# V and the scaled output rows of an RWKV-7 stage turned by 128x128 transpositions, with VectorE moving quarter blocks between the halves of the rows

## The chip, the cores and the metric

The kernel runs on one core of one Trainium2 chip. The metric is the device time of one execution in microseconds. The kernel before took 2906.01 us, the median of three runs from 2901.53 to 2912.75.

## What is computed

The reference is a decoder block on 512 positions of width 2048: RWKV-7 time mixing with 16 heads of 64 beside sliding-window attention, both merged by gates, then a gated convolutional feed-forward part. Only the time mixing is touched here. In the lines that matter, `v` is the value row of a head and `y` the state's output, which is centred and scaled per head and position:

```python
    def step(state, inp):
        r_t, k_t, v_t, w_t, ka_t, kb_t = inp
        sa = jnp.einsum('bhvk,bhk->bhv', state, ka_t)
        state = (state * w_t[:, :, None, :] + sa[..., None] * kb_t[:, :, None, :]
                 + v_t[..., None] * k_t[:, :, None, :])
        y = jnp.einsum('bhvk,bhk->bhv', state, r_t)
        return state, y
...
    mu = jnp.mean(y, axis=-1, keepdims=True)
    var = jnp.mean(jnp.square(y - mu), axis=-1, keepdims=True)
    y = ((y - mu) * lax.rsqrt(var + GN_EPS)).reshape(B, S, RW_DIM)
    y = y * gn_w.astype(f32) + gn_b.astype(f32)
```

`y` is linear in `v` along the head's columns, so the kernel takes the mean away from V at the start, and the mean of `y` is then zero.

## The kernel before

The program has four stages: projections of the input (`w_z`), with attention and the time mixing running beside them; the branch product; the output product (`w_out`); and the feed-forward part. The time mixing lies between about 330 and 1165 us. It works on eight pairs of heads, 128 rows each: `early(p)` makes the rows of a pair from three projections (k, r, v), `late(p)` runs the recurrence in eight chunks of 64 positions, and `final(p)` normalises the output and writes it out. They are called as late(p), early(p+1), final(p), then three projections for the gates.

Every projection is 48 matmuls of 128x512 (L262, L263, L264: high and low parts of the weights by high and low parts of the input). ScalarE makes the high part of a weight tile (`whi`, L245), VectorE the low part (`wlo`, L246); three buffers of each are in turn. These matmuls depend on nothing in the time mixing, and the framework's scheduler puts them between the time mixing's own instructions wherever it reckons that those would have to wait. In this text such matmuls are called filling. Each engine executes its queue in the order that the scheduler wrote; an instruction that waits holds all behind it.

Steps of one pair that the change touches:

- In `late`, ScalarE copies the halves of `vz` (128 channels x 512 positions) into the off-diagonal halves of `BV` (L668). Eight f32 products of 128x64 with the constant `cens` (an identity less 1/64) turn the chunks and centre them at once (L717 through `bulk_mm`, L714), and ScalarE copies the result from PSUM into `VV` (L715): positions of a chunk in the rows, channels in the columns, the head 1 of the pair in rows 0 to 63 and the head 0 in rows 64 to 127. Each f32 product of this kind shows as two MATMUL records in the trace.
- The next step, `GV` (L719, L714), needs `VV` and `OA`. Ahead of it on VectorE stand the masks of the chunk products (L694, sixteen of 128x256), and then, for each half g of the chunks, `tt` (L698, L699), `at_` (L705), the split into `AI` and `XIW` (L209) and `BT` (L710). `bulk` is a pool of three PSUM banks that all these products take in turn.
- In `final`, ScalarE copies y out of PSUM (`yt`, L802) and squares it (L808); VectorE sums (L810), takes the reciprocal root in thirteen small steps on 128x8 (`rsqrt_small`, L192 to L199), masks it for the two heads (`rs2`, L813), and makes two products of 128x512 (`yd`, L817). Eight f32 products with the constant `istack1` turn `yd` back (L820). Then come two products for the gate (L598), and VectorE finishes (L822, L825).

```python
                bulk_mm(VV, lambda n: BV[:, n], lambda n: K["cens"])
                GV = wk.tile([P, NCH, C], F32, name="GV", tag="yt")
                bulk_mm(GV, lambda n: OA[:, n], lambda n: VV[:, n])
```

## Time and profile before

| what | value |
|---|---|
| median of three runs | 2906.01 us |
| time of the profiled execution | 2907.66 us |
| its span | 2905.8 us |
| granted TensorE clock | 0.996 |
| TensorE (matmul) busy | 2850.9 us, 98% |
| VectorE busy | 1934.3 us, 67% |
| ScalarE busy | 1314.6 us, 45% |

A row of the timeline has the start in us, the time, the engine, the line, the operation, its operands and shapes, how many were merged, and in brackets the idle time ahead and what ended it. The time of a single matmul contains its way through the array; what a row of matmuls costs the queue is the distance from its start to the start of the next row. PE is TensorE, DVE VectorE, ACT ScalarE.

### The profile page before, as it was taken

The numbers are of one execution on the slowest core, as the hardware profiler recorded it, in microseconds if no ns is written. First come the engines' busy times: TensorE is split into PE (matmuls) and PEld (weight loads), VectorE is DVE, ScalarE is ACT, GpSimd is POOL, SyncE is SP. The second block draws the span as 40 slices with busy tenths as digits, with TensorE's granted clock in tenths as the row PEclk, the third lists the DMA queues.
The fourth block names the chain that finished last, engine by engine and source line by source line (L and its number), as shares of the span: only waits on it lengthen the run. The fifth ranks groups of instructions, "written<-read, shape, count | busy, mean of one in ns | idle before, by whom it ended". The sixth has DMA issues, their size and how long they took to land.

```text
span 2905.8 us, 47150 instructions
## 1 busy us (share of the span) xinstructions
PE 2850.9 (98%) x18162; PEld 2491.5 (86%) x18162; DVE 1934.3 (67%) x3314; ACT 1314.6 (45%) x2196; POOL 228.4 (8%) x304
## 2 busy tenths in 40 slices
PE   7999999999999999999999899999999999999999
PEld 6777778878878878788888899999999999888887
DVE  5555676666667665355668778777787777665555
ACT  4344344344334434322356455555555555544444
POOL 0001000000000000111000101110110100000000
PEclk9999999999999999999999999999999999999999
DMA  6855666566665666978787888888888888877775
GB/s 189 213 153 141 171 154 167 147 167 148 160 160 142 161 160 158 282 225 257 270 258 215 224 221 225 241 239 221 235 226 239 241 224 236 308 241 239 259 256 189
DMA packets 223729, 607.38 MB, mean 209 GB/s; under 512 B 24448, under 2 KB 44560, under 8 KB 222480
## 3 DMA queue, kind: packets, MB, share of 16 engines
q1 hardware_dynamic: 156096, 432.92, 45.9%
q0 software_dynamic: 36064, 132.14, 23.9%
q10 hardware_dynamic: 31344, 39.31, 3.9%
q8 instruction: 142, 2.33, 0.3%
q14 instruction: 83, 0.68, 0.1%
HBM read 554.66 MB, written 174.40 MB: 251 GB/s over the span
## 4 chain that ended last, share of the span: by engine, by line
PE 90%; DMA 4%; DVE 4%; issue 1%; ACT 1%; SPq 0%; DVEq 0%; ACTq 0%; POOLq 0%
PE X L1129 17%; PE X L996 10%; PE acc L263 10%; PE acc L262 10%; PE acc L264 10%; PE Y L996 8%; PE Y L1129 8%; PE Z L1129 4%; PE bulk L714 1%; PE bulk L770 1%; PE bulk L740 1%; PE bulk L690 1%; DMA raw<-in_w_up_dram 1%; PE mi L503 1%; PE acc L325 1%
## 5 line engine op out<-in xcount | busy, mean ns | idle before, releaser
L262 PE MATMUL acc<-xhi,whi 128*128 128x512 f32 x1120 | 453.6, 405 | 4.7 <-ACT whi L245 4.7
L264 PE MATMUL acc<-xhi,wlo 128*128 128x512 f32 x1120 | 451.5, 403 | 2.8 <-DVE wlo L246 2.8
L263 PE MATMUL acc<-xlo,whi 128*128 128x512 f32 x1120 | 453.0, 404 | 0.0
L245 ACT ACTIVATE whi<-raw 128x512 fp32r<-128x512 f32 x352 | 220.3, 629 | 499.2 <-PE acc L263 369.0
L246 DVE TENSOR_TENSOR wlo<-raw,whi 128x512 fp32r<-128x512 f32 x352 | 241.4, 689 | 233.5 <-ACT whi L245 227.7
L989 DVE TENSOR_TENSOR wlo<-raw,whi 128x1024 fp32r<-128x1024 f32 x210 | 257.0, 1224 | 205.4 <-ACT whi L988 204.3
L988 ACT ACTIVATE whi<-raw 128x1024 fp32r<-128x1024 f32 x210 | 222.6, 1060 | 291.4 <-PE X L996 152.5
L1129 PE MATMUL X<-b,whi 128*128 128x256 f32 x1472 | 269.1, 283 | 2.2 <-DVE u L1149 0.9
L1129 PE MATMUL X<-t,whi 128*128 128x256 f32 x1408 | 259.9, 285 | 9.9 <-DVE u L1149 9.4
L1112 DVE TENSOR_TENSOR wlo<-raw,whi 128x1024 fp32r<-128x1024 f32 x176 | 215.0, 1222 | 77.3 <-ACT whi L1111 77.0
L1129 PE MATMUL Y<-t,whi 128*128 128x256 f32 x1408 | 257.1, 283 | 0.0
L262 PEld LDWEIGHTS acc<-xhi,whi 128*128 128x128 f32 x1120 | 211.9, 189 | 44.4 <-ACT whi L245 5.5
L264 PEld LDWEIGHTS acc<-xhi,wlo 128*128 128x128 f32 x1120 | 211.9, 189 | 42.0 <-DVE wlo L246 4.0
L263 PEld LDWEIGHTS acc<-xlo,whi 128*128 128x128 f32 x1120 | 211.8, 189 | 37.3 <-issue 1.8
L1111 ACT ACTIVATE whi<-a 128x1024 fp32r<-128x1024 f32 x132 | 139.4, 1056 | 216.5 <-DVE a L1105 214.5
L1129 PEld LDWEIGHTS X<-b,whi 128*128 128x128 f32 x1472 | 229.5, 192 | 3.0 <-issue 2.3
L1129 PEld LDWEIGHTS X<-t,whi 128*128 128x128 f32 x1408 | 221.8, 194 | 10.5 <-DVE u L1149 6.9
L1129 PEld LDWEIGHTS Y<-t,whi 128*128 128x128 f32 x1408 | 219.6, 192 | 0.0
L1129 PE MATMUL X<-b,wlo 128*128 128x256 f32 x736 | 208.5, 283 | 2.1 <-DVE wlo L1112 2.1
L1112 DVE TENSOR_TENSOR wlo<-a,whi 128x1024 fp32r<-128x1024 f32 x132 | 161.7, 1225 | 67.6 <-ACT whi L1111 67.0
L1129 PE MATMUL X<-t,wlo 128*128 128x256 f32 x704 | 200.4, 285 | 0.0
L1129 PE MATMUL Y<-t,wlo 128*128 128x256 f32 x704 | 199.2, 283 | 0.0
(769 smaller groups left out, 6007.1 us busy)
## 6 DMA issues: line engine op xcount, KB each, us to landing
raw<-in_w_up_dram SPq DMA_DIRECT2D x180, 512.0 KB, 4.9
raw<-in_w_z_dram SPq DMA_DIRECT2D x288, 256.0 KB, 4.0
s_dn<-in_w_dn_dram POOLq DMA_DIRECT2D x88, 512.0 KB, 6.5
raw<-in_w_up_dram POOLq DMA_DIRECT2D x88, 512.0 KB, 8.4
raw<-s_dn SPq DMA_DIRECT2D x88, 512.0 KB, 4.1
raw<-in_w_dn_dram SPq DMA_DIRECT2D x66, 512.0 KB, 3.6
a<-in_w_up_dram SPq DMA_DIRECT2D x48, 512.0 KB, 4.4
s_dn<-in_w_dn_dram SPq DMA_DIRECT2D x44, 512.0 KB, 4.7
```

What stands on the lines that cost most here:

```text
L245: pin(act.activation(hi, raw, AF.Copy))
L246: pin(dve.tensor_tensor(lo, raw, hi.bitcast(F32), op=ALU.subtract))
L262: pe.matmul(acc, whi[:, j], xhi[:, k], start=first, stop=False)
L263: pe.matmul(acc, whi[:, j], xlo[:, k], start=False, stop=False)
L264: pe.matmul(acc, wlo[:, j], xhi[:, k], start=False, stop=last)
L325: pin(pe.matmul(heads[i][:, hs], l, r[:, k, hs], start=h == 0 and k + j == 0, stop=k == NK - 1 and j == 2, skip_group_check=True))
L988: act.activation(whi, wr, AF.Copy)
L989: dve.tensor_tensor(wlo, wr, whi.bitcast(F32), op=ALU.subtract)
L996: pe.matmul(dst, l[:, q, ts], r[:, es], start=fst and j == 0, stop=lst and j == 2, skip_group_check=True)
L1111: pin(act.activation(hi, t, AF.Copy))
L1112: pin(dve.tensor_tensor(lo, t, hi.bitcast(F32), op=ALU.subtract))
L1129: pin(pe.matmul(ps, l[:, k], r[:, k], start=start and k + i == 0, stop=last and i == 2, skip_group_check=True))
```

## The change

V: four transpositions of 128x128 turn `vz` as it stands, so that `BV`, its copies and its clearing go. A transposed block has 128 positions, that is two chunks, in its rows, and both heads in its columns. VectorE sums the 64 columns of each head and position out of PSUM (`vm`, 128x8), multiplies by -1/64, and adds that in four operations of 64x4x64, each of which reads one half of the rows of PSUM and writes one half of the rows of `VV`. In two of the four the halves differ.

Output: the mask `rs2` goes. Four operations of 64x4x64 instead of two of 128x512 make `yd`, now with 128 positions in the rows and both heads in the columns; again two of the four move between the halves. Four transpositions of 128x128 turn it back, instead of eight products. The constants `istack1` and `cens` go.

```diff
-                    act.activation(BV[hs, :, ol:oh], vz3[hs], AF.Copy)
...
-                bulk_mm(VV, lambda n: BV[:, n], lambda n: K["cens"])
+                ps = bulk()
+                for t in range(NT):
+                    ts = slice(t * P, (t + 1) * P)
+                    pe.transpose(ps[:, ts], vz[:, ts], ident)
+                vm = wk.tile([P, NCH], F32, name="vm", tag="vm")
+                dve.reduce_sum(vm, r3(ps), axis=AX.X)
+                dve.tensor_scalar(vm, vm, -1.0 / HD, None, op0=ALU.mult)
+                for a, (fl, fh) in enumerate(HV):
+                    for h in range(2):
+                        ol, oh = HV[1 - h]
+                        dve.tensor_tensor(VV[ol:oh, a::2], r3(ps)[fl:fh, h::2],
+                                          vm[fl:fh, h::2].unsqueeze(2).to_broadcast([C, NT, C]), op=ALU.add)
...
-                rs2 = wk.tile([P, NCH, 2], F32, name="rs2", tag="rs2")
-                dve.tensor_tensor(rs2, rs.unsqueeze(2).to_broadcast([P, NCH, 2]),
-                                  K["sel2"].unsqueeze(1).to_broadcast([P, NCH, 2]), op=ALU.mult)
-                yd = wk.tile([P, NCH, 2, C], F32, name="yd", tag="ko")
-                for h in range(2):
-                    dve.tensor_tensor(yd[:, :, h], yt, rs2[:, :, h : h + 1].to_broadcast([P, NCH, C]), op=ALU.mult)
+                yd = wk.tile([P, NT, 2, C], F32, name="yd", tag="ko")
+                for a, (al, ah) in enumerate(HV):
+                    for h, (lo, hi) in enumerate(HV):
+                        dve.tensor_tensor(yd[al:ah, :, h], yt[lo:hi, a::2],
+                                          rs[lo:hi, a::2].unsqueeze(2).to_broadcast([C, NT, C]), op=ALU.mult)
                 ps = bulk()
-                for n in range(NCH):
-                    pe.matmul(r3(ps)[:, n], yd[:, n].rearrange("p h c -> p (h c)"), K["istack1"], start=True, stop=True)
+                for t in range(NT):
+                    pe.transpose(ps[:, t * P : (t + 1) * P], yd[:, t].rearrange("p h c -> p (h c)"), ident)
```

The scheduler orders the engines anew. Three places around the start of the third pair follow (the output step is that of the second pair, which ends just ahead of it); line numbers of the changed kernel are smaller by two to five up to `late` and larger by five to six behind it (L694 becomes L689, L714 becomes L709, L820 becomes L825).

TensorE at V, before: the eight products for V, four filling matmuls, then `GV` and the transpositions of `BKE`.

```order
L714 MATMUL bulk<-cst,BV 128x64 x8
L264 MATMUL acc<-xhi,wlo 128x512
L262 MATMUL acc<-xhi,whi 128x512
L263 MATMUL acc<-xlo,whi 128x512
L264 MATMUL acc<-xhi,wlo 128x512
L714 MATMUL bulk<-VV,OA 128x64 x8
L724 MATMUL bulk<-ident,BKE 128x128 x4
```

TensorE at V, now: behind the four transpositions stand thirty filling matmuls, of which the last five are shown, and `GV` comes as one product, the transpositions of `BKE`, and the other seven.

```order
L715 MATMUL bulk<-ident,vz 128x128 x4
...
L261 MATMUL acc<-xlo,whi 128x512
L262 MATMUL acc<-xhi,wlo 128x512
L260 MATMUL acc<-xhi,whi 128x512
L261 MATMUL acc<-xlo,whi 128x512
L262 MATMUL acc<-xhi,wlo 128x512
L709 MATMUL bulk<-VV,OA 128x64
L730 MATMUL bulk<-ident,BKE 128x128 x4
L260 MATMUL acc<-xhi,whi 128x512
L709 MATMUL bulk<-VV,OA 128x64 x7
```

So the filling between V and `GV` went from four matmuls to thirty (28 in the first pair). It was taken from ahead of the first chunk products (64 there before, 45 now) and from ahead of the turning of `yd` (39 before, 30 now). In the whole queue there are 416 stretches of such matmuls before, and 399 now.

VectorE at V, before: from the first `XIW` to the end of the second half g. Ahead of these rows stand the sixteen masks, `tt` twice, `at_`, `tt`, `tt`, `BX` and `tt`.

```order
L209 TENSOR_TENSOR XIW<-tt,XIW 128x256
L209 TENSOR_TENSOR AI<-at__5611,AI 128x512
L710 TENSOR_TENSOR BT<-AI,cst 128x512 x2
L699 TENSOR_TENSOR tt<-tt,cst 128x256
L705 SCALAR_TENSOR_TENSOR at__5629<-bulk,cst 128x512
L708 TENSOR_SCALAR BX<-tt 64x4x64
L209 TENSOR_TENSOR XIW<-tt,XIW 128x256
L246 TENSOR_TENSOR wlo<-raw,whi 128x512
L209 TENSOR_TENSOR AI<-at__5629,AI 128x512
L710 TENSOR_TENSOR BT<-AI,cst 128x512 x2
L744 TENSOR_TENSOR half__5706<-half__5706,bulk 128x8x32
```

VectorE at V, now: the first six rows behind the masks (up to the first `BX`) are the same as before; then come `AI`, `XIW`, two `BT` and `tt` of the first half, and then these rows.

```order
L700 SCALAR_TENSOR_TENSOR at__5617<-bulk,cst 128x512
L694 TENSOR_TENSOR tt<-tt,cst 128x256
L717 TENSOR_REDUCE vm<-bulk 128x8
L207 TENSOR_TENSOR AI<-at__5617,AI 128x512
L207 TENSOR_TENSOR XIW<-tt,XIW 128x256
L703 TENSOR_SCALAR BX<-tt 64x4x64
L705 TENSOR_TENSOR BT<-AI,cst 128x512 x2
L718 TENSOR_SCALAR vm<-vm 128x8
L244 TENSOR_TENSOR wlo<-raw,whi 128x512
L722 TENSOR_TENSOR VV<-bulk,vm 64x4x64 x4
L244 TENSOR_TENSOR wlo<-raw,whi 128x512 x2
```

The sum `vm` stands behind the second `at_`, and `VV` stands last, behind the second `BT` and one `wlo`. That `wlo` is the one that the twenty-seventh and the thirtieth of the filling matmuls use.

VectorE in `final`, before: from the sum of squares to the middle of the root.

```order
L810 TENSOR_REDUCE ssy<-gn 128x8
L666 SCALAR_TENSOR_TENSOR BAR<-kk,Et 64x8x64
L192 TENSOR_SCALAR rq_5283<-ssy 128x8
L246 TENSOR_TENSOR wlo<-raw,whi 128x512
L193 TENSOR_SCALAR rq_5285<-rq_5283 128x8
L667 TENSOR_TENSOR BAR<-rz,Et 64x8x64
L194 TENSOR_SCALAR rq_5284<-rq_5285 128x8
L195 TENSOR_SCALAR rq_5283<-rq_5283 128x8
L685 TENSOR_TENSOR BKE<-BKK,ee 128x1024
L197 TENSOR_TENSOR rq_5285<-rq_5284 128x8
L246 TENSOR_TENSOR wlo<-raw,whi 128x512
L198 TENSOR_TENSOR rq_5285<-rq_5285,rq_5283 128x8
```

VectorE in `final`, now: the products `BAR` and one `wlo` stand ahead of the sum, and `BKE` further ahead.

```order
L662 SCALAR_TENSOR_TENSOR BAR<-kk,Et 64x8x64 x2
L663 TENSOR_TENSOR BAR<-rz,Et 64x8x64 x2
L244 TENSOR_TENSOR wlo<-raw,whi 128x512
L816 TENSOR_REDUCE ssy<-gn 128x8
L190 TENSOR_SCALAR rq_5277<-ssy 128x8
L191 TENSOR_SCALAR rq_5279<-rq_5277 128x8
L192 TENSOR_SCALAR rq_5278<-rq_5279 128x8
L193 TENSOR_SCALAR rq_5277<-rq_5277 128x8
L195 TENSOR_TENSOR rq_5279<-rq_5278 128x8
```

Behind these come the other eight small steps with one more `wlo` among them, and then `yd` four times. On ScalarE the square of `yt` now stands behind one `whi`; before, it followed the copy of `yt` at once.

## The prediction

> **What bounds the kernel now.** I read the page's first lines, the windows of one pair each, TensorE's waits between 330 and 1165 us, and then the timelines of the two places where V and the output are turned. The page first, its span, busy times and the chain that ended last:

> ```profile
> span 2905.8 us, 47150 instructions
> PE 2850.9 (98%) x18162; PEld 2491.5 (86%) x18162; DVE 1934.3 (67%) x3314; ACT 1314.6 (45%) x2196; POOL 228.4 (8%) x304
> PE 90%; DMA 4%; DVE 4%; issue 1%; ACT 1%; SPq 0%; DVEq 0%; ACTq 0%; POOLq 0%
> ```

> The window of the third pair (engine busy times, granted clock, DMA share, GB/s), and TensorE's longest wait of the stage with its count and longest case:

> ```profile
> 553.00:658.00 105.00, 104.11 (x687) 85.10 (x686) 71.22 (x171) 44.31 (x98) 8.12 (x11) 1.00 0.61 154
> PE bulk L820 <- DVE yd L817: 5.8, 8, 0.8
> ```

> TensorE is full in this stage: 104.1 of 105 us, at full clock. Filling matmuls stand wherever the time mixing would wait, so an instruction that TensorE loses is time gained, and a place where its queue stops is time lost. Averages of the other engines say little; what counts is whether TensorE comes to a place before VectorE is done.

> **TensorE's work.** The timeline at V, at the turning of `yd`, and at a run of eight transpositions (start, time):

> ```profile
> 533.80 0.39 PE L263 MATMUL acc<-xlo,whi 128*128 128x512 f32 x1
> 534.95 2.00 PE L820 MATMUL bulk<-cst,yd 128*128 128x64 f32 x16 [0.76 <-DVE yd L817]
> 536.79 1.94 PE L598 MATMUL bulk<-ads,wl 128*128 128x512 f32 x4
> ...
> 560.75 1.89 PE L714 MATMUL bulk<-cst,BV 128*128 128x64 f32 x16
> 562.45 0.48 PE L264 MATMUL acc<-xhi,wlo 128*128 128x512 f32 x1
> 562.76 0.40 PE L262 MATMUL acc<-xhi,whi 128*128 128x512 f32 x1
> 563.00 0.40 PE L263 MATMUL acc<-xlo,whi 128*128 128x512 f32 x1
> ...
> 576.89 1.03 PE L770 MATMUL bulk<-ident,BX 128*128 128x128 f32 x8
> 577.76 0.19 PE L740 MATMUL bulk<-XIW,AI 128*128 128x64 f16 x1
> ```

> From start to next start, V costs 562.45 - 560.75 = 1.70 us and the output 536.79 - 534.95 = 1.84 us. Eight transpositions cost 577.76 - 576.89 = 0.87, four of them 0.44. So a pair loses 1.70 + 1.84 - 0.88 = 2.66 us of TensorE, and eight pairs 21.3 us. A filling matmul costs 0.23 us, the first behind f32 work 0.31; the order has 17 stretches of filling fewer, worth 17 x 0.08 = 1.4 us.

> [...]

> **VectorE at V.** Two groups of ScalarE go (busy time, mean ns | idle ahead):

> ```profile
> L668 ACT ACTIVATE BV<-vz 64x512 f32<-64x512 f32 x16 | 10.0, 625 | 1.5 <-DVE vz L532 1.4
> L715 ACT ACTIVATE VV<-bulk 128x512 f32<-128x512 f32 x8 | 4.8, 598 | 15.2 <-PE bulk L714 15.2
> ```

> ScalarE loses two copies to `BV` and one to `VV` per pair; VectorE gets a sum, a small product and four additions, all ahead of `GV`. Before, V went 0.6 us through an idle ScalarE and TensorE did not wait. The price of the new place is the length of VectorE's queue up to `VV` against what TensorE has to do meanwhile. VectorE's rows in the third pair, from the first mask on, with the distance between starts as the price:

> ```profile
> 554.35 0.42 DVE L694 TENSOR_TENSOR BX<-bulk,cst 128x256 f32<-128x256 f32 x1
> 554.69 0.41 DVE L694 TENSOR_TENSOR OA<-bulk,cst 128x256 f32<-128x256 f32 x1
> ...
> 559.66 0.84 DVE L698 TENSOR_TENSOR tt<-BX,cst 64x256 f32<-64x256 f32 x2
> 560.53 0.69 DVE L705 SCALAR_TENSOR_TENSOR at__5611<-bulk,cst 128x512 f32<-128x512 f32 x1
> 561.14 0.42 DVE L699 TENSOR_TENSOR tt<-tt,cst 128x256 f32<-128x256 f32 x1
> 561.47 0.41 DVE L698 TENSOR_TENSOR tt<-BX,cst 64x256 f32<-64x256 f32 x1
> 561.89 0.29 DVE L708 TENSOR_SCALAR BX<-tt 64x256 f32<-64x256 f32 x1
> 562.11 0.42 DVE L698 TENSOR_TENSOR tt<-BX,cst 64x256 f32<-64x256 f32 x1
> ...
> 564.13 0.69 DVE L209 TENSOR_TENSOR AI<-at__5611,AI 128x512 f16<-128x512 f32 x1
> 564.74 1.29 DVE L710 TENSOR_TENSOR BT<-AI,cst 128x512 f16<-128x512 f16 x2
> 565.94 0.42 DVE L699 TENSOR_TENSOR tt<-tt,cst 128x256 f32<-128x256 f32 x1
> ...
> 568.19 0.42 DVE L209 TENSOR_TENSOR XIW<-tt,XIW 128x256 f16<-128x256 f32 x1 [0.91 <-ACT XIW L208]
> 568.53 0.68 DVE L246 TENSOR_TENSOR wlo<-raw,whi 128x512 fp32r<-128x512 f32 x1
> 569.13 0.68 DVE L209 TENSOR_TENSOR AI<-at__5629,AI 128x512 f16<-128x512 f32 x1
> ```

> Up to 562.11 the order is unchanged, and so is what sets the start (the chunk products and a `wlo` ahead of them). From there the new queue to the second `VV` is: AI 0.61, XIW 0.34, two BT 1.20, tt 0.42, at_ 0.61, tt 0.34, the sum 0.71 (as the sum of squares, 526.71 to 527.42 below), AI 0.61, XIW 0.34, BX 0.22, two BT 1.20, the small product 0.17, `wlo` 0.60, and two additions 0.84 (as two `tt`). That is 8.2 us, with no idle time, since ScalarE's halves of these splits are done by then: it has lost its copy of V, behind which `XIW` stood. So the first two of four additions, all that the first product of `GV` needs, end near 570.3.

> TensorE comes there earlier. V starts at 560.75 as before (the rows ahead of it have the same counts), takes 0.44, and thirty filling matmuls 0.31 + 29 x 0.23 = 6.9: it wants `GV` at 568.1. It stops even before that, at the twenty-seventh, whose `wlo` stands right ahead of `VV`, but the total is set by `VV`: 570.4 - 568.1 = 2.3 us per pair. Behind it stand the filling, all chunk products, and through them everything else of the pair.

> No row of before shows a VectorE operation that reads one half of the rows and writes the other. The lower bound is the 0.33 us of a mask that follows another (554.35 to 554.69), the upper one twice the 0.42 of `tt`; I take 0.42, since `tt` has the same 64x256.

> [...]

> I take 2.5 us. [...] Lost are 8 x 2.5 = 20 us.

> **VectorE at the output.** Rows of the second pair, TensorE first, then ScalarE, then VectorE:

> ```profile
> 525.06 0.48 PE L264 MATMUL acc<-xhi,wlo 128*128 128x512 f32 x1
> 525.29 0.60 ACT L802 ACTIVATE yt<-bulk 128x512 f32<-128x512 f32 x1 [0.75 <-PE bulk L800]
> 526.74 0.63 ACT L245 ACTIVATE whi<-raw 128x512 fp32r<-128x512 f32 x1 [0.19 <-PE acc L263]
> 525.29 0.68 DVE L667 TENSOR_TENSOR BAR<-rz,Et 64x512 f32<-64x512 f32 x1 [0.48 <-PE bulk L800]
> 525.99 0.69 DVE L665 TENSOR_TENSOR BKK<-k,Ei 64x512 f32<-64x512 f32 x1
> 526.71 0.69 DVE L810 TENSOR_REDUCE ssy<-gn 128x8 f32<-128x512 f32 x1
> 527.42 0.69 DVE L666 SCALAR_TENSOR_TENSOR BAR<-kk,Et 64x512 f32<-64x512 f32 x1
> 532.92 0.17 DVE L198 TENSOR_TENSOR rq<-rq,rq 128x8 f32<-128x8 f32 x1
> 533.12 0.17 DVE L199 SCALAR_TENSOR_TENSOR rq<-rq,rq 128x8 f32<-128x8 f32 x1
> 533.60 1.29 DVE L817 TENSOR_TENSOR yd<-yt,rs 128x512 f32<-128x512 f32 x2
> ```

> Before, 39 filling matmuls end 0.92 us too early (1.15 between 533.80 and 534.95, less 0.23). Now 30 stand there: TensorE, from 525.06, wants `yd` at 525.06 + 0.31 + 29 x 0.23 = 532.0. VectorE: two `BAR` 1.40 from 525.29, `wlo` 0.60 (its `whi` is ready by 526.6), the sum 0.71, to 528.0; the small steps 0.20 each where one needs the last (532.92 to 533.12), twelve of these, 2.4; one `wlo` more, 0.5 net; so `yd` starts at 530.9 and, at 4 x 0.42, ends at 532.6. The wait is 0.65 us instead of 0.92, since the queue now holds some 3 us less of other work behind the sum: 0.25 us gained per pair, 2 us in all. With 0.33 a piece the gain is 5 us; with twice 0.42 for the two that cross it is a loss of 5.

> **What costs nothing.** The ScalarE copies removed (idle there 0.75 us and more per step), the clearing of `BV` at the stage's start on POOL, and 128 fewer columns of constants are hidden under a full TensorE; without that cover the copies would be worth (10.0 + 4.8) / 8 = 1.85 us a pair. No DMA moves but the weights' loads, with the filling that uses them.

> **The sum.** -21.3 - 1.4 + 20 - 2 = -4.7 us. The profiled execution took 2907.66 us (span 2905.8) and would take 2903; it lies 1.65 above the median, so the forecast is 2906.0 - 4.7 = 2901.3 us. About 0.5% (14.5 us) is what a measurement here can tell from no change; 4.7 is less.

> **The rivals.** *The wait at V is filled.* If VectorE's new queue is no longer than the thirty filling matmuls, only the two gains stay: -21.3 - 1.4 - 2 = -25 us, 2881. For it: the scheduler put thirty there, where it reckons that `VV` is ready, and at V before it reckoned well. Against it: at `yd` it reckoned 0.92 us too little, and from the last mask (559.66) to 570.3 stand 10.6 us of measured VectorE time, against 7.3 of TensorE's. Chance 0.17.

> *The output becomes the stop.* Nine filling matmuls that covered VectorE are gone. If `yd` still ends as late as before, 9.6 us behind 525.29 where TensorE has freed the rows (533.60 + 1.29 = 534.89), because `BAR` and `wlo` now stand ahead of the sum, the wait is 2.9 us instead of 0.65, 18 us more: 2919; and with it the two crossings of `yd` at twice the price, another 0.84 us, 7 us: 2926, slower by 0.7%. It decides above 9.8 us of that chain, where the total passes +0.5%. For it: the chain is VectorE's longest run of small dependent steps. Against it: the order leaves 0.5 us of foreign work inside. Chance 0.1.

> *The change doesn't do what it says*: transpositions in two passes like the f32 products. Sixteen records for eight products against eight for eight transpositions speak against; it would take 0.88 us per pair back, 7 us: 2908. Chance 0.03.

> **How the numbers follow.** The forecast, a stop of 1.5 to 3.3 us at V, has 0.7. Its own ends are 8 us better and 6 worse at V, and 3 better to 7 worse at the output, not both at once: 2892 to 2910. The range of 8 in 10 reaches down to most of the first rival and up to the start of the second: 2882 to 2917. Faster by over 0.5% (below 2891.5): 0.17 and a lower tail of 0.08, 0.25. Slower by over 0.5% (above 2920.5): 0.1. Within: 0.65.

> **What would show it.** Right: L715 four records at 0.11; TensorE idle some 2.5 us on `wlo` or `VV` in each pair, eight times; below 1 us on `yd`; pairs some 0.6 us closer together than before. Wrong: no wait at V (the first rival), a wait above 2 us at `yd` (the second), or additions with crossing halves longer than 0.42.

## The result, and the profile after

The changed kernel takes 2918.14 us, the median of five runs from 2916.86 to 2925.21; the kernel before took 2906.65 us beside it, also the median of five. The ratio is 1.0049, with a 95% interval of 1.0037 to 1.0061. The forecast was 4.7 us less; it came out 11.5 us more, just outside the range. The page of the changed kernel, its span, busy times and the chain that ended last:

```profile
span 2916.4 us, 46799 instructions
PE 2843.1 (97%) x17970; PEld 2485.0 (85%) x17970; DVE 1955.5 (67%) x3370; ACT 1304.5 (45%) x2172; POOL 227.9 (8%) x303
PE 90%; DVE 6%; DMA 2%; ACT 1%; issue 1%; ACTq 0%; SPq 0%; DVEq 0%; POOLq 0%
```

TensorE is busy for 7.8 us less (2850.9 before) in a span that is 10.6 us longer, and VectorE's share of the chain has grown from 4% to 6%. The waits of TensorE between 330 and 1165 us say where:

```profile
PE acc L262 <- DVE wlo L244: 22.7, 9, 3.5
PE bulk L825 <- DVE yd L821: 4.6, 7, 0.7
PE bulk L685 <- DVE bon L649: 1.9, 1, 1.9
```

The first row is the stop at V: 3.5 us in the first pair, 2.54 in each of the other seven, and one wait of 1.4 us ahead of the pairs. TensorE's timeline in the third pair, from the transpositions of `vz` to `GV`:

```profile
562.24 0.60 PE L715 MATMUL bulk<-ident,vz 128*128 128x128 f32 x4
562.59 0.48 PE L262 MATMUL acc<-xhi,wlo 128*128 128x512 f32 x1
...
568.16 0.39 PE L260 MATMUL acc<-xhi,whi 128*128 128x512 f32 x1
568.39 0.39 PE L261 MATMUL acc<-xlo,whi 128*128 128x512 f32 x1
571.32 0.50 PE L262 MATMUL acc<-xhi,wlo 128*128 128x512 f32 x1 [2.54 <-DVE wlo L244]
571.65 0.39 PE L260 MATMUL acc<-xhi,whi 128*128 128x512 f32 x1
...
572.36 0.34 PE L709 MATMUL bulk<-VV,OA 128*128 128x64 f32 x2
572.53 0.61 PE L730 MATMUL bulk<-ident,BKE 128*128 128x128 f32 x4
572.89 0.48 PE L260 MATMUL acc<-xhi,whi 128*128 128x512 f32 x1
573.21 1.67 PE L709 MATMUL bulk<-VV,OA 128*128 128x64 f32 x14
574.72 0.61 PE L730 MATMUL bulk<-ident,BKE 128*128 128x128 f32 x4
```

The four transpositions cost 0.35 us. The filling stops at the twenty-seventh matmul for the `wlo` that stands ahead of `VV` in VectorE's queue. VectorE at that place, and TensorE where `yd` is turned back:

```profile
570.51 0.16 DVE L718 TENSOR_SCALAR vm<-vm 128x8 f32<-128x8 f32 x1
570.58 0.68 DVE L244 TENSOR_TENSOR wlo<-raw,whi 128x512 fp32r<-128x512 f32 x1
571.29 1.75 DVE L722 TENSOR_TENSOR VV<-bulk,vm 64x256 f32<-64x256 f32 x4
```

```profile
541.13 0.39 PE L262 MATMUL acc<-xhi,wlo 128*128 128x512 f32 x1
542.17 0.66 PE L825 MATMUL bulk<-ident,yd 128*128 128x128 f32 x4 [0.66 <-DVE yd L821]
542.67 1.88 PE L594 MATMUL bulk<-ads,wl 128*128 128x512 f32 x4
```

All of this is much as foreseen. What was not foreseen shows when two pairs of the same kernel are put side by side, the third and the fourth, each from one first chunk product to the next (columns as in the prediction: TensorE's busy time comes first, the granted clock is third from the end):

```profile
554.60:659.27 104.67, 101.42 (x663) 82.36 (x662) 73.87 (x178) 43.24 (x96) 8.12 (x11) 1.00 0.62 157
659.27:765.47 106.20, 102.94 (x662) 83.87 (x661) 73.87 (x178) 43.24 (x96) 8.40 (x11) 0.98 0.61 154
```

The same instructions, the same idle time (3.25 and 3.26 us), and yet the fourth pair takes 1.53 us longer, 1.52 of it TensorE's busy time, at a granted clock of 0.98 instead of 1.00. The trace's record of the granted clock knows two values, 1.00 and 0.50, and half lasts 3.413, 6.827 or 10.240 us in this kernel (2.717 at the end, where the program stops). The stretch around the stop in the fourth pair, in steps of 3.41 us that meet where that record changes:

```profile
669.69:673.11 3.42, 3.42 (x17) 2.78 (x15) 3.38 (x7) 1.87 (x5) 0.00 (x0) 1.00 0.26 50
673.11:676.52 3.41, 0.87 (x4) 0.48 (x3) 3.34 (x9) 0.46 (x1) 0.00 (x0) 1.00 0.00 0
676.52:679.93 3.41, 3.41 (x15) 3.09 (x14) 2.44 (x5) 0.38 (x1) 0.00 (x0) 0.50 0.39 99
679.93:683.35 3.42, 3.36 (x25) 2.83 (x25) 0.00 (x0) 2.15 (x6) 1.04 (x2) 1.00 0.83 279
```

The stop of 2.54 us lies in the second window, and the whole third window runs at half clock. What ran there in the third pair at full clock (0.34, 0.61 and 1.67 us above) took longer here:

```profile
677.42 0.53 PE L709 MATMUL bulk<-VV,OA 128*128 128x64 f32 x2
677.73 1.06 PE L730 MATMUL bulk<-ident,BKE 128*128 128x128 f32 x4
...
679.02 2.11 PE L709 MATMUL bulk<-VV,OA 128*128 128x64 f32 x14
```

Below, a window at half clock that follows such a stop is called a drop. Seven of the eight stops at V were followed by one; only the third was not, and the drop behind the eighth lasted three windows. In all the changed kernel has 17 half-clock windows, the kernel before 6 (the last one at the very end of each not counted). The feed-forward part has six instead of three of them, and is 4.8 us longer with the same waits:

```profile
1567.90:2479.90 912.00, 898.47 (x7457) 897.24 (x7458) 720.86 (x864) 470.89 (x637) 94.24 (x111) 0.99 0.85 230
```

```profile
1574.90:2491.70 916.80, 902.90 (x7456) 901.34 (x7457) 721.12 (x865) 470.80 (x638) 94.01 (x111) 0.99 0.84 228
```

The first row is the kernel before, the second the changed one.

### The profile page after: what moved, and what is told of

It is laid out like the page before. It is cut to its first block, busy times and chain, and to the rows that moved or that the text cites. A ratio compares the mean times of both kernels' runs of the same rounds, so it can differ in the third digit from the quotient of the medians.

```text
span 2916.4 us, 46799 instructions
## 1 busy us (share of the span) xinstructions
PE 2843.1 (97%) x17970; PEld 2485.0 (85%) x17970; DVE 1955.5 (67%) x3370; ACT 1304.5 (45%) x2172; POOL 227.9 (8%) x303
## 4 chain that ended last, share of the span: by engine, by line
PE 90%; DVE 6%; DMA 2%; ACT 1%; issue 1%; ACTq 0%; SPq 0%; DVEq 0%; POOLq 0%
PE X L1134 17%; PE X L1001 11%; PE acc L262 10%; PE acc L260 10%; PE acc L261 10%; PE Y L1001 8%; PE Y L1134 8%; PE Z L1134 4%; PE bulk L709 1%; PE bulk L776 1%; PE bulk L746 1%; PE mi L501 1%; DMA raw<-in_w_z_dram 1%; PE acc L323 1%; PE bulk L594 1%; PE scp L467 1%
## 5 line engine op out<-in xcount | busy, mean ns | idle before, releaser
L262 PE MATMUL acc<-xhi,wlo 128*128 128x512 f32 x1120 | 454.4, 406 | 22.7 <-DVE wlo L244 22.7
L262 PEld LDWEIGHTS acc<-xhi,wlo 128*128 128x128 f32 x1120 | 213.3, 190 | 64.7 <-DVE wlo L244 27.3
```

The lines of the kernel that those rows point to most:

```text
L262: pe.matmul(acc, wlo[:, j], xhi[:, k], start=False, stop=last)
```

## The experiments

Three theories stood at the start. **A**: the loss is made at V, by a stop (VectorE's queue is longer than the filling) and by the drop of the clock behind it. **B**: the quarter-block work on VectorE costs more than it saves, wherever it stands. **C**: the difference is made behind the pairs. After the first four runs a sharper form of A was to be tested, **the grid**: the clock is set for windows of 3.413 us that lie fixed in time, so a stop makes a drop or not by where it falls. Each experiment ran beside the kernel before (medians from 2904.75 to 2905.65 us in four sessions). Column by column: the ratio with its interval, TensorE's stop at V per pair, how many of the eight stops were followed by a drop, all half-clock windows, and a usual distance from pair to pair.

| run | median us | ratio | stop | drops | windows | pair us |
|---|---|---|---|---|---|---|
| before | 2906.65 | | none | | 6 | 105.07 |
| after | 2918.14 | 1.0049 (1.0037 to 1.0061) | 2.54 | 7 | 17 | 106.0 to 106.2, once 104.67 |
| e1 output part alone | 2896.97 | 0.9973 (0.9963 to 0.9984) | none | | 7 | 104.0 |
| e2 V part alone | 2914.27 | 1.0028 (1.0018 to 1.0039) | 2.53 | 2 | 8 | 105.8 |
| e3 V block earlier | 2880.26 | 0.9914 (0.9901 to 0.9928) | none | | 5 | 102.0 |
| e4 16-bit mask | 2895.03 | 0.9963 (0.9950 to 0.9975) | 1.47 | 0 | 7 | 103.55 |
| e5 ten transpositions more | 2911.99 | 1.0024 (1.0015 to 1.0034) | 2.54 | 2 | 9 | 105.67 |
| e6 e3 with the mask | 2881.40 | 0.9916 (0.9902 to 0.9929) | none | | 7 | 102.2 |
| e7 before with the mask | 2903.36 | 0.9990 (0.9981 to 0.9999) | none | | 8 | 104.8 |
| e8 e3 with ten more | 2888.25 | 0.9942 (0.9928 to 0.9955) | none | | 6 | 103.0 |
| e9 31 more | 2943.20 | 1.0129 (1.0114 to 1.0143) | 2.54 | 8 | 13 | 109.5 |
| e10 43 more | 2943.90 | 1.0133 (1.0119 to 1.0146) | 2.54 | 2 | 12 | 109.29 |
| e11 V block still earlier | 2883.20 | 0.9924 (0.9911 to 0.9938) | none | | 6 | 102.3 |
| e12 after once more | 2920.91 | 1.0052 (1.0038 to 1.0066) | 2.55 | 8 | 21 | 106.1 |

**e1, the output part alone.** The kernel before, with these lines of the change:

```diff
-                rs2 = wk.tile([P, NCH, 2], F32, name="rs2", tag="rs2")
...
+                for a, (al, ah) in enumerate(HV):
+                    for h, (lo, hi) in enumerate(HV):
+                        dve.tensor_tensor(yd[al:ah, :, h], yt[lo:hi, a::2],
...
+                for t in range(NT):
+                    pe.transpose(ps[:, t * P : (t + 1) * P], yd[:, t].rearrange("p h c -> p (h c)"), ident)
```

> The kernel before with the output part alone: the scaled rows turned by four transpositions, V left as it was. Theory A (the loss is made at V: TensorE stops 2.5 us in each pair because VectorE's queue is longer than the filling, and in most pairs the granted clock then drops to 0.50 for a window of 3.4 us) expects no stop at V, no half-clock window inside the pairs beyond the one or two of the kernel before, and 8 x (1.84 - 0.44) = 11 us less: near 2896 us, ratio 0.996. Theory B (the quarter-block work on VectorE costs more than it saves wherever it stands, in both parts alike) expects this half to be slower too: 2908 to 2913 us, ratio 1.001 to 1.002. Theory C (the difference is not made in the pairs but in the feed-forward stage behind them) expects the pairs to be some 1.4 us closer together and the total still at or above that of the kernel before.

It took 2896.97 us, as A expects. The wait at `yd` grew a little, from 5.8 us in all to 7.5:

```profile
PE bulk L819 <- DVE yd L815: 7.5, 8, 1.0
```

Half of the change is a gain; B and C fall for this half.

**e2, the V part alone.** The kernel before, with the change's lines at V:

```diff
-                    act.activation(BV[hs, :, ol:oh], vz3[hs], AF.Copy)
...
-                bulk_mm(VV, lambda n: BV[:, n], lambda n: K["cens"])
+                    pe.transpose(ps[:, ts], vz[:, ts], ident)
...
+                dve.reduce_sum(vm, r3(ps), axis=AX.X)
```

> The kernel before with the V part alone, the output left as it was. Theory A expects the stop at V of 2.5 to 2.7 us in each pair and the half-clock window behind most of them: -10 us of TensorE's work, +21 us of stops, +8 to 10 us of clock, near 2925 us, ratio 1.006 to 1.007, with six or seven half-clock windows of 3.4 us or more inside the pairs. Theory B expects it to take about half of what the full change takes: near 2912 us, ratio 1.002, with the rest in the output part.

It took 2914.27 us, which by its time alone is nearer to B. But the stop is what A said:

```profile
PE acc L263 <- DVE wlo L245: 22.9, 9, 3.5
```

Only the drops are missing: two instead of six or seven. The parts alone come to -8.7 and +8.6 us, the whole to +11.5. The whole has nine half-clock windows more than e2 (17 against 8), and at 1.3 us each they would make up the 11.6 us that the sum of the parts lacks. The windows around its fourth stop show why one stop of 2.53 us may have none:

```profile
676.77:680.18 3.41, 2.35 (x11) 1.62 (x9) 3.38 (x7) 1.77 (x4) 0.00 (x0) 1.00 0.00 0
680.18:683.59 3.41, 1.93 (x12) 1.63 (x13) 3.29 (x9) 0.07 (x1) 0.00 (x0) 1.00 0.18 47
683.59:687.01 3.42, 3.37 (x25) 2.83 (x25) 1.12 (x2) 2.02 (x6) 1.04 (x2) 1.00 0.48 124
```

The same stop, but a boundary cuts it into 1.05 and 1.48 us, and the clock stays full. From here the grid was a theory of its own.

**e3, the V block earlier.** The full change; the whole block of V is written ahead of the loop over the halves g, right behind the masks (the expectations of e3, e6 and e8 call this place "ahead of the chunk products"; the first chunk products and their sixteen masks stand ahead of it):

```diff
+                ps = bulk()
+                for t in range(NT):
+                    ts = slice(t * P, (t + 1) * P)
+                    pe.transpose(ps[:, ts], vz[:, ts], ident)
...
                 for g in range(2):
                     ns = slice(g * HN, (g + 1) * HN)
...
-                ps = bulk()
-                for t in range(NT):
-                    ts = slice(t * P, (t + 1) * P)
-                    pe.transpose(ps[:, ts], vz[:, ts], ident)
```

> The full change with the seven VectorE instructions of V written ahead of the chunk products instead of behind them: between the masks and the two BT products nothing stands ahead of the additions any more, so that VV is ready long before GV is asked for. The work is the same, only its place differs. Theory A expects no stop at V, TensorE's clock full through the pairs, and the whole gain of 21 us with 2 us at yd: 2880 to 2888 us, ratio 0.991 to 0.994. Theory B expects no better than 2912 us, since the same instructions are paid for. Theory C expects the pairs about 2.5 us closer together and most of that lost again behind them.

It took 2880.26 us, the fastest of all, with the same operations as the changed kernel. TensorE no longer waits at V; this is its longest wait in the pairs, and a pair:

```profile
PE bulk L825 <- DVE yd L821: 4.8, 8, 0.6
```

```profile
532.91:634.86 101.95, 101.27 (x663) 82.63 (x661) 74.31 (x178) 43.07 (x95) 8.12 (x11) 1.00 0.61 160
```

A pair is 105.07 - 101.95 = 3.12 us shorter than before; the prediction's gains without the stop, (21.3 + 1.4 + 2) / 8, are 3.09. So the work was priced rightly, and B and C fall altogether.

**e4, the mask in 16 bits.** The changed kernel; the queue at V gets shorter and nothing moves:

```diff
+            t16 = bd.tile([P, P], F16, name="t16")
+            dve.tensor_copy(t16, K["t1bd"])
...
-                        dve.tensor_tensor(BT[:, i, ns], AI[:, i, ns], mb("t1bd", HN), op=ALU.mult)
+                        dve.tensor_tensor(BT[:, i, ns], AI[:, i, ns], t16.unsqueeze(1).to_broadcast([P, HN, P]), op=ALU.mult)
```

> The changed kernel with the mask of the four BT products held as 16-bit numbers too, so that all operands of these products are 16 bits wide; the order of the instructions stays the same. It shortens the queue ahead of VV without moving anything. If the product goes from 0.61 us a start to about 0.33 us, theory A expects the stop at V to fall from 2.6 to about 1.5 us a pair (9 us less), and with it fewer or no half-clock windows (up to 10 us less): 2898 to 2910 us, ratio 0.997 to 1.001. If the product takes 0.61 us as before, the time stays that of the changed kernel, 2918 us, and nothing is said on the theories. Theory B expects 2914 us or more: only the shorter products that TensorE might wait for elsewhere count.

The product went from 686 to 421 ns (shortest, median and longest of four of them in the changed kernel's third pair, then of two in this kernel's, and then this kernel's wait at V):

```profile
L705 DVE TENSOR_TENSOR BT<-AI,cst x4: 684/686/691, 564.7 to 569.9; 128x512 f16<-128x512 f16 x4
```

```profile
L707 DVE TENSOR_TENSOR BT<-AI,t x2: 418/421/424, 560.0 to 560.4; 128x512 f16<-128x512 f16 x2
```

```profile
PE acc L262 <- DVE wlo L244: 12.2, 8, 1.9
```

Four times 0.265 is 1.06, and the stop fell by 1.07, from 2.54 to 1.47 us: it is the length of VectorE's queue. No drop is left, though five of the seven stops of 1.47 us lie whole in one window. The time fell by 23 us, to 2895.03, more than the 8 to 20 expected: 8.6 us of stops, and ten half-clock windows fewer.

**e5, ten transpositions for nothing.** The changed kernel; each pair does more work, far from V:

```diff
-                                pe.transpose(ps[:, j], BX[:, g * HN + j], ident)
+                                for again in range(6 if m == LEVELS[1] and g == 0 and j < 2 else 1):
+                                    pe.transpose(ps[:, j], BX[:, g * HN + j], ident)
```

> The changed kernel with ten transpositions per pair made once more for nothing (the first two of a level's transposition of the block matrix are made six times instead of once): 10 x 0.109 = 1.09 us of TensorE work added to each pair, far from V and from the output; the order is the same otherwise. It tests whether the drops of the clock hang on where the stop at V lies in a fixed grid of windows of 3.413 us. In the changed kernel a pair without a drop takes 104.67 us, 30.67 windows; with 1.09 us more it takes 105.76, 30.98 windows, so that the stop comes back at the same place of the grid in each pair, and a drop (some 1.3 us more, 0.4 of a window) moves it out of the place that makes one. Theory A with the grid: at most three pairs with a half-clock window; the drops saved (5 x 1.3 us) pay for most of the 8.7 us added: 2918 to 2923 us. Theory A without a grid (any stop of 2.5 us makes a drop, but for chance): seven drops as before and 8.7 us more: near 2927 us. If the added work hides or lengthens the stop, the wait at V shows it; I expect it at 2.5 us as before.

The kernel does 8 us more work and takes 6 us less, 2911.99. The stop is unchanged:

```profile
PE acc L262 <- DVE wlo L244: 22.2, 9, 3.5
```

The time lies below the 2918 to 2923 us expected. Two stops of eight were followed by a drop. From the second stop to the sixth the part of it in one window crept up, as pairs of 30.96 windows make it: 1.45, 1.57, 1.72, 1.87, 2.01 us, and the 2.01 brought the drop. The gain is larger than I had reckoned (five drops saved; the record has eight windows fewer in all).

**e6, e3 with the 16-bit mask.** Both edits together.

> The full change with the V block ahead of the chunk products, and the mask of the BT products as 16-bit numbers as well. With no stop at V, a VectorE that is 8 x 4 x 0.27 = 8.5 us shorter should be worth nothing there. Theory A: 2878 to 2882 us, as without the 16-bit mask, ratio 0.991. If VectorE's time were worth something everywhere (theory B), another 8 us less: 2872 us.

It took 2881.40 us, 1.1 more than e3: the 8.5 us of VectorE were worth nothing here, where TensorE does not wait at V.

**e7, the kernel before with the 16-bit mask.**

> The kernel before with the 16-bit mask alone: the control for what the mask gives where no stop stands at V. Theory A: 0 to -3 us (the longest wait there is the 0.7 us at yd, which it does not reach), 2903 to 2906 us, ratio 0.999 to 1.000. If it gains 10 us or more here, the gain of the mask in the changed kernel says nothing on the stop at V.

It took 2903.36 us beside 2905.47, as expected: the mask by itself gives 2 us, and the rest of the 23 us of e4 is a matter of the stop.

**e8, e3 with the ten transpositions.**

> The control for the ten added transpositions: the same ten in the kernel with the V block ahead of the chunk products, where no stop stands at V and the clock stays full. Theory A, with a grid or without: 8 x 1.09 = 8.7 us more than that kernel's 2880 us: 2887 to 2891 us, ratio 0.994.

It took 2888.25 us, 8.0 more than e3. Without a stop the added work costs 8.0 of the 8.7 us that it was priced at.

**e9 and e10, 31 and 43 transpositions for nothing.** As e5, with other counts:

```diff
-                                for again in range(6 if m == LEVELS[1] and g == 0 and j < 2 else 1):
+                                for again in range((17, 16)[j] if m == LEVELS[1] and g == 0 and j < 2 else 1):
```

The second kernel has 23 and 22 in place of 17 and 16.

> The changed kernel with 31 transpositions for nothing in each pair instead of ten, at the same place. Ten made a pair without a drop 1.00 us longer (104.67 to 105.67), so 31 make it 3.1 to 3.25 us longer: 107.8 to 107.9 us, 31.6 windows of 3.413 us, the same remainder as in the changed kernel itself; with a drop of 1.3 us it is 32.0 windows, so that the next stop falls where the last one fell. Theory A with the grid: the drops come back, in five or more of the eight pairs, and the time is that of the changed kernel plus all of the work, 2918 + 8 x 3.2 = 2944 us. Theory A without a grid, by which the ten transpositions broke the drops because there was more work between the stops: few drops here too, 2912 + 8 x 2.15 = 2929 us.

> The same with 43 transpositions, one window more than in the run with ten: a pair without a drop takes 109.0 to 109.2 us, 31.9 to 32.0 windows. Theory A with the grid: the drops go again (one to three pairs with one), and twelve transpositions more than in the run with 31 (9.9 us) cost only 2 to 5 us: 2912 + 8 x 3.4 = 2939 us, up to 2945 with a third drop, and the mean clock 0.004 above that of the run with 31. Without a grid: 10 us above the run with 31.

The drops are back in e9, behind all eight stops, and gone again in e10 but for two. Twelve transpositions more in each pair, some 10 us by the price in e8, cost 0.7 us: 2943.20 against 2943.90. From the first chunk product of the first pair to the last of the eighth both take 777.5 us. Without a grid the second had to be 10 us slower. One execution of each was profiled; the mean granted clock points the same way in every execution, 0.989 to 0.992 in the four of e9 and 0.993 to 0.996 in the four of e10.

**e11, the V block still earlier.** As e3, with the block ahead of the products whose result the masks take.

> The full change with the V block still earlier, ahead of the products whose result the masks take: VectorE has its sum and its four additions done before the first mask. Theory A: no stop at V and no half-clock windows in the pairs, as with the block between products and masks: 2878 to 2888 us, ratio 0.991 to 0.994. A rival: the block now delays the masks and the chunk products behind them, by the 2.5 us that its six instructions take, and a wait of up to 2.5 us stands there: up to 2900 us.

It took 2883.20 us, a little more than e3; the rival's wait did not come.

**e12, the changed kernel once more.**

> The changed kernel once more, for a second profile of it. The grid theory says that its pairs hold themselves in the place of the grid that makes drops (a pair with a drop takes 31.1 windows): five or more of the eight stops followed by a drop again, and 2914 to 2924 us. If the drops were chance, their number would be anywhere between none and eight. The feed-forward part took 916.6 us in the first profile, with six half-clock windows in it. If that is its place in the grid by chance, it has two to six this time, at 910 to 917 us; if the change itself does something to that part, it has six again and 916 us or more.

It took 2920.91 us. All eight stops were followed by a drop, so the drops are a property of this kernel and no accident of one run. The mean granted clock of every execution fits: 0.987 to 0.992 in the ten of this kernel, 0.993 to 0.997 in the nine of e5. The feed-forward part took 916.0 us and has six half-clock windows again, so its loss is not chance either: in both profiles its first long wait, 2.1 us for a `wlo`, begins 394.6 us behind the last half-clock window ahead of that part (which follows a wait for a `whi`, not a stop at V), at the same place of the grid. In e10 it does so as well, and there the part takes 916.3 us; in the kernel before it is 398.4 us, 0.5 us later in its window, and 911.8 us. With two windows (e9) it took 910.4. That the last half-clock window sets the place for the feed-forward part was read from four profiles and not tried by an edit.

**The 56 stops of the seven runs that have them** (after, e2, e4, e5, e9, e10, e12), cut at the grid's boundaries (multiples of 3.413 us from a kernel's first half-clock window behind 340 us; later ones lie on it within 0.02 us), by the longest idle time that one window got of them:

| idle of the stop in one window | stops | followed by a drop |
|---|---|---|
| up to 1.73 us | 25 | 0 |
| 1.82, 1.87, 1.93 us | 3 | 1 (1.82) |
| 1.95 us and more | 28 | 28 |

(1.93 is the third stop of the changed kernel.) The border is not sharp by this measure: in e9 and e12 a wait of 1.85 us ahead of the first pair, whole in one window, was followed by half clock too. It holds beyond the stops: of all windows of the fourteen profiles from 30 us on that ran at full clock themselves, none of the 11554 with up to 1.69 us without matmuls was followed by one at half clock, each of the 66 with 1.95 us and more was, and the 21 between went both ways. Of the 29 drops 20 lasted one window, four two, and five three; behind these five, 0.51 to 0.59 us of the same stop fell into the drop's own window, behind the 20 at most 0.47.

A drop of one window costs 1.3 to 1.5 us of a pair (105.97 and 106.20 against 104.67), one of three 4.2 (108.87 in e12). And a pair with a drop takes 106.0 to 106.2 us in the changed kernel, 31.1 windows: the next stop falls 0.2 to 0.4 us later in its window than the last one, and a stop of 2.54 us has room for several such steps before it leaves the place that makes drops. In e2 a pair without a drop takes 31.0 windows, and stays where it is harmless. So two kernels with the same stop may differ: one whose pairs with a drop last nearly a whole number of windows keeps its drops, one whose pairs without a drop do so keeps free of them.

## Why the prediction was wrong

- **TensorE's work: right.** V went from 1.70 to 0.35 us, the output from 1.84 to 0.50 (542.67 - 542.17), together 2.69 per pair where 2.66 was forecast. e3 shows the whole of it in the time.
- **The price of quarter blocks that cross the halves: right.** 0.42 us was taken; the two groups of 32 have these means, half of each cross, and the longest single one took 0.428 us:

```profile
L722 DVE TENSOR_TENSOR VV<-bulk,vm 64x256 f32<-64x256 f32 x32 | 13.5, 422 | 0.7
L821 DVE TENSOR_TENSOR yd<-yt,rq 64x256 f32<-64x256 f32 x32 | 13.4, 419 | 1.1
```

- **The stop at V: right in mechanism, a little small.** 2.5 us were forecast. TensorE loses 571.32 - 568.39 - 0.23 = 2.70 us, and 0.1 more on the first matmul behind the stop (0.33 to the next start instead of 0.23); in the first pair, with 28 filling matmuls, 1 us more. That is 8 x 2.8 + 1 = 23.4 us instead of 20. The rows of before gave 2.3 us; the 0.2 on top of them, and the ends of 1.5 and 3.3 us, were the author's estimate, and no run shows them as terms of their own. What the third pair shows is that the fourteen steps from `AI` to the second addition take 8.42 us (563.72 to 572.14) where 8.2 were worked out. The stop ends with the `wlo`, and not with `VV` as the prediction had it: the first two of its four additions end near 571.29 + 0.85 = 572.14, and `GV` comes at 572.36 without waiting.
- **The wait at `yd`: a little too small.** 0.65 was forecast instead of 0.92, both by distance between starts. By that measure it is 542.17 - 541.13 - 0.23 = 0.81 (the 0.66 in the row is the idle time alone, to be set against 0.76 before), so 0.1 us a pair is gained instead of 0.25, or 1 us in all instead of 2.
- **The sum: here it failed.** "-21.3 - 1.4 + 20 - 2 = -4.7" holds for a pair at full clock, as the third shows (104.67 against 105.07, -0.40, where -0.59 was forecast). It has no term for the granted clock. The first part of the prediction took the clock of the stage before, 1.00, as given: "TensorE is full in this stage: 104.1 of 105 us, at full clock". The change that it went on to price puts eight stops into that stage. With the stop and the wait at `yd` at their measured sizes the sum is -0.3 us; by the third pair (8 x -0.40, and the 1 us of the first) it is -2.2. The span grew by 10.6, so 11 to 13 us are left, for eleven half-clock windows more. That is 1.0 to 1.2 us each, a little less than the 1.3 to 1.5 of a pair; the 2 to 5 us or so between the two were not traced further.
- **The rivals.** The first rival was argued against with 10.6 us of VectorE from 559.66 on and 7.3 of TensorE, but the second count begins at 560.75; from 559.66 on TensorE has 8.4, and the difference is 2.2, as in the forecast's own working (2.3). The wait at V was not filled, the output did not become the stop, and the four transpositions of V show as four records, 0.35 us from their start to the filling. The time came near to that of the second rival, 2919, for another reason. Missing was a rival by which the stop also slows what comes behind it. The kernel before had what was needed to see it, ahead of the first pair, where TensorE waits 2.76 us for a `wlo`; two windows of its profile and the matmul behind the wait:

```profile
331.17:334.58 3.41, 0.65 (x4) 0.22 (x3) 2.12 (x4) 0.53 (x1) 0.00 (x0) 1.00 0.21 76
334.58:338.00 3.42, 3.42 (x9) 2.68 (x10) 3.42 (x6) 0.00 (x0) 0.00 (x0) 0.50 0.64 171
```

```profile
334.47 0.73 PE L264 MATMUL acc<-xhi,wlo 128*128 128x512 f32 x1 [2.76 <-DVE wlo L246]
```

## What to carry to other kernels

When a change puts a stop of 2 us or more on a full TensorE, price the clock behind it too: here it was half a stop more (1.3 to 1.5 us for 2.54) for a window at half clock. Whether it was due hung on where the stop fell in windows of 3.413 us: 28 of 28 stops with 1.95 us or more in one window were followed by half clock, none of 25 with up to 1.73. So two kernels with the same stop of 2.54 us differed by some 9 us of clock (e9 and e10, 0.7 us apart with some 10 us of work between them). A change whose work is priced rightly can lose by the place it is written at: the same operations, moved ahead of the products that shared VectorE with them, turned +0.5% into -0.9%. If a kernel gets faster with work added (e5: 6 us, with ten transpositions more per pair), look at the granted clock before anything else.
